# Context and latent keys together in 512-column products, latent values moved to the second phase

## The chip, the cores and the metric

The kernel runs on one core of a Trainium2 chip. The metric is device time in microseconds from start to end of one execution, the median of three runs. Matrix products are done by TensorE (PE, with its weight loads listed apart as PEld). VectorE (DVE) and ScalarE (ACT) split weights and do all elementwise work, GpSimd (POOL) starts some loads and fills borders, SyncE (SP) starts the large loads.

## The reference, cut to what matters

One layer of a hybrid backbone. 256 latent tokens and 256 context tokens, 4096 channels, float32.

```
mod_l = silu(c) @ w_ada + b_ada ;  mod_c = silu(c_ctx) @ w_ada + b_ada     # w_ada: 4096 x 12288
hl = rmsnorm(xl) * (1 + sc_l) + sh_l ;  hc = rmsnorm(xc) * (1 + sc_c) + sh_c
a_val, a_glu, a_gate, r_x, r_gate, q, k, v, c_gate = split(h @ w_in)        # w_in: 4096 x 13312
A: conv module over a_val, a_glu          (latents only)
B: two-way gated recurrence over r_x      (context first, its last state starts the latents)
C: attention of 16 heads, head size 128: q of latents; k, v of latents (windowed) and of context
out = rmsnorm(xl + g_l * (concat(A * silu(a_gate), B * silu(r_gate), C * silu(c_gate)) @ w_out))
```

From the context only r_x (1024 columns), k (2048) and v (2048) are needed; from the latents all nine parts.

## The kernel before, in words

**Products.** A float32 product is made of three passes in float32r. `weights` (L327 to L340) loads up to 4 tiles of 128 contraction rows by 512 output columns (1 MB) through SP's queue into one of 3 buffers `raw`. Then, for two tiles at a time (a pair), ACT copies them into `hi` (L338) and DVE subtracts to `lo` (L339), in 3 buffers each. The activations `h` are kept in two parts likewise. A product adds hi·hi, hi·lo and lo·hi. There are two forms. `gemm_cm` (L342 to L359) is channel-major: the weights are the stationary operand and the 256 tokens of one stream move through, so a matmul has 256 columns; for 512 output columns that is 4 x 3 matmuls of 256 columns for each contraction tile and stream. `gemm_tm` (L361 to L374) is token-major: 128 tokens of `h` are stationary and 512 weight columns move, 3 matmuls of 512 columns for each contraction tile and 128 tokens.

**Phase 1** (L482 to L552) goes over the contraction in blocks of 1, 2, 3, 3, 3, 4, 4, 4, 4, 4 tiles, because the modulation that `h` needs is itself computed during it: units of `w_ada` loads and small products (`ada_units`, L217) are put between the pairs by `background`, at a rate that grows with the weight it is called with. For each block there are ten chunks of 512 columns in the order r0 k0 v0 k1 v1 k2 v2 k3 r1 v3 (in the last block both r first). r is made for both streams by `gemm_cm` (4 PSUM banks), k for the context alone by `gemm_cm` (2 banks), v for both streams by `gemm_tm` (4 banks). `spill` (L499) adds the banks to sums `acc` in SBUF, on DVE. After the ninth chunk of a block, `make_h` (L314 to L324) makes the next block's `h` of both streams, four DVE and two ACT instructions of 256 columns a tile: `CH` for the context, `LH` for the latents.

**Recurrences.** Eight pieces (`recurrence`), one for each head; five are put behind chunks of the last block (`REC1`), three between chunks of the second phase. They share three tiles a direction and two for gate weights.

**Phase 2** (L558 to L742) uses `LH` only, over the whole contraction of 32 tiles: conv inputs (c0, c1), four attention groups of four heads (a0 to a3: k, q, gate, each by `gemm_cm`, then `attention`), gates and pointwise products. In `attention` the scores are two matmuls of 256 keys, context and latents (L593, L594). Phase 3 is the output projection by `gemm_tm`.

**Order and space.** The program orders the instructions of each engine before the run, by priority (`hp` marks what is urgent) and by its own estimate of times; on the chip each engine goes strictly through its list. A tile waits for space until all uses of an earlier tile in its slot are over. SBUF is shared out as 75 pages of 2 KB a partition (X, CH, LH, acc, and nearly every temporary tile) beside the weight buffers. PSUM has 5 banks for the large products and 3 for all else.

Of the kernel before, what the change touches and what calls it, by code (L numbers as in the profile page):

```python
# [10 lines left out]
F32 = mybir.dt.float32  # L11
# [6 lines left out]
P = 128  # L18
D = 4096
KT = D // P  # L20
T = 256
# [4 lines left out]
# blocks of the contraction in the first phase, in tiles of 128  # L26
BLOCKS = [1, 2, 3, 3, 3, 4, 4, 4, 4, 4]
# from this block on, every second one's shift is summed on the vector engine
PAIRED = 8
# pages of 2 KB, buffers of weights as loaded and as split  # L30
NPG, NRAW, NHI = 75, 3, 3
# tiles of the contraction kept for the second half of the last chunk
HELD = 12
# urgency of what the tensor engine waits for
HP = 200000
# rates of the loads that go beside the products, by phase
ADA_A, ADA_B, CAP = 2.15, 1.2, 4.0
G1, G2, G3 = 0.4, 0.3, 0.4
# chunks of the last block that a recurrence follows; order of the second phase
# [5 lines left out]
def tile_hybrid_layer(ctx: ExitStack, tc: tile.TileContext, x, c, cctx_tok, c_ctx, w_ada, b_ada,  # L45
# [13 lines left out]
    def background(weight):  # L59
        """emits queued units of loads between those of the products, at the set rate"""  # L60
        bg["credit"] = min(bg["credit"] + bg["rate"](weight), CAP)
        while bg["q"] and bg["credit"] >= 2.0:
            bg["credit"] -= 2.0
            bg["q"].pop(0)()

    def page(shape, dt=F32, name="pg"):
        uid[0] += 1
        return pg.tile(shape, dt, name=f"{name}_{uid[0]}", tag="pg", bufs=NPG)

# [53 lines left out]
    # silu(c), silu(c_ctx) as channel columns, padded to 32 stationary columns  # L123
# [31 lines left out]
    def accumulate(k, w, n, which):  # L155
        """gacc[b] += silu(vector b)[k] * w on the vector engine"""
# [101 lines left out]
    def rsqrt(y, v, t):  # L258
        """y = v ** -0.5, the table's root refined by a Newton step"""
# [52 lines left out]
    CH, LH = {}, {}  # L312

    def make_h(k):  # L314
        h = page([P, 512], name="h")
        CH[k] = page([P, 2, T], F32R, name="ch")
        LH[k] = page([P, 2, T], F32R, name="lh")
        for s, dst in ((1, CH[k]), (0, LH[k])):
            sl = slice(0, T) if s == 1 else slice(T, 2 * T)
            V.scalar_tensor_tensor(h[:, sl], X[k][:, sl], modG[:, k, s:s + 1], R[:, sl], ALU.mult, ALU.mult)  # L320
            A.activation(dst[:, 0], h[:, sl], AF.Identity, bias=modS[:, k, s:s + 1])
            V.scalar_tensor_tensor(dst[:, 1], h[:, sl], modS[:, k, s:s + 1], dst[:, 0].bitcast(F32),
                                   ALU.add, ALU.subtract)
# [529 lines left out]
```

## Time and profile before

| | us |
|---|---|
| median of 3 runs (2374.56 to 2380.82) | 2377.08 |
| profiled execution, first to last instruction | 2371.5 |
| PE busy | 2315.1 |
| PEld busy | 2034.4 |
| DVE busy | 1580.3 |
| ACT busy | 945.7 |

The profiled execution's time is known as its span, 2371.5 us; the median of the runs is 5.6 us above, which takes in what lies ahead of the first and behind the last instruction. A matmul's row in the trace lasts longer than its distance to the next one, because matmuls are pipelined: what a matmul costs is read from the distance between the starts of successive rows.

### The profile page before, as it was taken

The page shows a single profiled execution, that of the slowest core. Times are in us where ns is not written, and L with a number is a line of the kernel's source. Part 1 is how long each engine was busy: PE and PEld are TensorE (multiplying, and loading weights), DVE is VectorE, ACT ScalarE, POOL GpSimd, SP SyncE. Part 2 cuts the span into 40 slices and gives each one's busy share as a digit, 9 for nine tenths or more (in the row PEclk, how much of TensorE's full clock was granted, in tenths as well). Part 3 has the DMA queues.
Part 4 walks back from the last instruction along what each step waited for, and adds up shares of the span by engine and source line. Part 5 has one row for each costly group of instructions (what it writes and reads, how often), then busy time and mean ns, then how long its engine had stood idle before and what let it go on. Part 6 is the DMA issues. An engine that isn't in the chain of part 4 may idle for free.

```text
span 2371.5 us, 38433 instructions
## 1 busy us (share of the span) xinstructions
PE 2315.1 (98%) x16013; PEld 2034.4 (86%) x16013; DVE 1580.3 (67%) x2289; ACT 945.7 (40%) x1228; POOL 95.8 (4%) x150
## 2 busy tenths in 40 slices
PE   6899999999999999999999999999999999999997
PEld 4667777777788998999999899999999999888886
DVE  4465545445778779987879596955766666665555
ACT  5322212222223246886433343344444434434444
POOL 0000000000000001000000101101001001000000
PEclk9999999999999999999999999999999999999999
DMA  9888788877877544656776767767576678775664
GB/s 312 270 279 272 254 298 298 295 266 252 295 269 258 192 163 174 222 183 213 245 233 203 188 215 202 204 215 188 182 245 171 207 265 301 264 263 187 191 192 173
DMA packets 293461, 551.27 MB, mean 232 GB/s; under 512 B 10959, under 2 KB 52647, under 8 KB 293287
## 3 DMA queue, kind: packets, MB, share of 16 engines
q1 hardware_dynamic: 287856, 536.91, 66.1%
q0 software_dynamic: 4480, 11.54, 4.3%
q8 instruction: 125, 2.05, 0.3%
q10 hardware_dynamic: 951, 0.37, 0.1%
q14 instruction: 49, 0.40, 0.0%
HBM read 544.58 MB, written 4.19 MB: 231 GB/s over the span
## 4 chain that ended last, share of the span: by engine, by line
PE 83%; DMA 8%; DVE 4%; ACT 3%; issue 1%; SPq 0%; DVEq 0%; ACTq 0%
PE gcm L355 48%; PE gtm L371 9%; PE gtm L372 8%; PE gtm L370 8%; PE psa L217 5%; DMA raw<-in_w_ada_dram 4%; DMA raw<-in_w_in_dram 3%; DVE lo L339 2%; PE y L614 1%; ACT hi L338 1%; DMA xp<-in_ctx_dram 1%; DVE gacc L245 1%; PE pt L607 1%; PE sc L593 0%; PE sc L594 0%
## 5 line engine op out<-in xcount | busy, mean ns | idle before, releaser
L339 DVE TENSOR_TENSOR lo<-raw,hi 128x1024 fp32r<-128x1024 f32 (+1 forms) x630 | 747.4, 1189 | 556.8 <-ACT hi L338 552.9
L338 ACT CAST hi<-raw 128x1024 fp32r<-128x1024 f32 (+1 forms) x630 | 640.1, 1022 | 1171.9 <-PE gcm L355 492.8
L355 PE MATMUL gcm<-lh,hi 128*128 128x256 f32 x5632 | 1069.5, 285 | 2.9 <-ACT hi L338 2.8
L355 PEld LDWEIGHTS gcm<-lh,hi 128*128 128x128 f32 x5632 | 896.8, 192 | 18.3 <-issue 13.4
L355 PE MATMUL gcm<-lh,lo 128*128 128x256 f32 x2816 | 796.2, 285 | 4.2 <-DVE lo L339 4.0
L355 PEld LDWEIGHTS gcm<-lh,lo 128*128 128x128 f32 x2816 | 537.8, 192 | 11.6 <-DVE lo L339 5.8
L355 PE MATMUL gcm<-ch,hi 128*128 128x256 f32 x1536 | 326.6, 287 | 3.4 <-ACT hi L338 2.3
L355 PEld LDWEIGHTS gcm<-ch,hi 128*128 128x128 f32 x1536 | 259.0, 191 | 36.3 <-issue 27.8
L245 DVE SCALAR_TENSOR_TENSOR gacc<-raw,scol,gacc 128x512 f32<-128x512 f32 x248 | 185.8, 749 | 49.6 <-DMA raw<-in_w_ada_dram 47.1
L355 PE MATMUL gcm<-ch,lo 128*128 128x256 f32 x768 | 217.6, 286 | 0.0
L371 PE MATMUL gtm<-lo,mix 128*128 128x512 f32 x488 | 192.0, 393 | 0.1
L372 PE MATMUL gtm<-hi,mix 128*128 128x512 f32 x488 | 190.1, 390 | 0.0
L370 PE MATMUL gtm<-hi,mix 128*128 128x512 f32 x488 | 171.1, 390 | 0.0
L355 PEld LDWEIGHTS gcm<-ch,lo 128*128 128x128 f32 x768 | 146.5, 191 | 12.8 <-issue 9.0
L217 PE MATMUL psa<-raw,cpad 128*32 128x512 f32 (+3 forms) x1216 | 132.5, 521 | 7.9 <-DMA raw<-in_w_ada_dram 7.8
L499 DVE TENSOR_TENSOR acc<-acc,gcm 128x512 f32<-128x512 f32 x144 | 96.1, 682 | 37.7 <-PE gcm L355 37.1
L371 PEld LDWEIGHTS gtm<-lo,mix 128*128 128x128 f32 x488 | 91.6, 188 | 20.5 <-DVE lo L339 1.3
L370 PEld LDWEIGHTS gtm<-hi,mix 128*128 128x128 f32 x488 | 91.5, 188 | 19.2
L499 DVE TENSOR_TENSOR acc<-acc,gtm 128x512 f32<-128x512 f32 x144 | 94.3, 680 | 19.9 <-PE gtm L372 19.7
L372 PEld LDWEIGHTS gtm<-hi,mix 128*128 128x128 f32 x488 | 91.7, 188 | 18.4
L673 DVE SCALAR_TENSOR_TENSOR cv<-upad,cols,cv 128x256 f32<-128x256 f32 x240 | 105.6, 483 | 0.0
L371 PE MATMUL gtm<-lo,ch 128*128 128x512 f32 x256 | 102.2, 399 | 0.2 <-DVE lo L339 0.2
(218 smaller groups left out, 2107.9 us busy)
## 6 DMA issues: line engine op xcount, KB each, us to landing
raw<-in_w_in_dram SPq DMA_DIRECT2D x210, 1024.0 KB, 5.2
raw<-in_w_ada_dram SPq DMA_DIRECT2D x156, 1024.0 KB, 5.5
raw<-in_w_out_dram SPq DMA_DIRECT2D x61, 1024.0 KB, 5.5
raw<-in_w_ada_dram SPq DMA_DIRECT2D x48, 768.0 KB, 5.9
raw<-in_w_in_dram SPq DMA_DIRECT2D x30, 768.0 KB, 6.1
raw<-in_w_in_dram SPq DMA_DIRECT2D x10, 512.0 KB, 5.4
xp<-in_ctx_dram SPq DMA_DIRECT2D x16, 256.0 KB, 5.8
xp<-in_x_dram SPq DMA_DIRECT2D x16, 256.0 KB, 5.4
```

What stands on the lines that cost most here:

```text
L217: nc.tensor.matmul(st["ps"][32 * q:32 * q + 32, :W], cpad[k // 16][:, k % 16, :], raw[:, j, :], start=(k < 4), stop=(k >= KT - 4))
L245: V.scalar_tensor_tensor(st["a"], raw[:, j], s, st["a"], ALU.mult, ALU.add)
L338: A.copy(hi[:, :n], raw[:, o:o + n])
L339: V.tensor_sub(lo[:, :n], raw[:, o:o + n], hi[:, :n].bitcast(F32))
L355: nc.tensor.matmul(banks[r // 2][:, (r % 2) * T:(r % 2) * T + T], w[:, j, nt * P:(nt + 1) * P], movs[m][k][:, part], start=first, stop=las ...
L370: nc.tensor.matmul(banks[b], hh, wh[:, j], start=first, stop=False)
L371: nc.tensor.matmul(banks[b], hh, wl[:, j], start=False, stop=False)
L372: nc.tensor.matmul(banks[b], hl, wh[:, j], start=False, stop=last)
L499: V.tensor_add(acc[key, i], acc[key, i], b)
L607: nc.tensor.transpose(ps[:, kt * T + qt * P:kt * T + qt * P + P], Ps[qt][:, (2 * kp + kt) * P:(2 * kp + kt + 1) * P], ident)
L614: nc.tensor.matmul(ps[:, :T], acc[("v", h // 4), kt][:, i * P:(i + 1) * P], Ps[kt // 2][:, (kt % 2) * T:(kt % 2) * T + T], start=(kt == 0) ...
L673: V.scalar_tensor_tensor(o, upad[n][:, tap:tap + T], cw(tap, n), o, ALU.mult, ALU.add)
```

## The change

r and k of phase 1 are made for both streams by one new function, `gemm_both`. The two streams' parts of `h` of one contraction tile now lie side by side in a 4 KB tile `H4` ([part, stream, token]), so that one matmul moves 512 columns. v of phase 1 is made for the context only. In phase 2 each attention group makes the latents' v by `gemm_tm` in the place where it made the latents' k by `gemm_cm`. `keep_h` copies the latents' half of `H4` into a page after the fifth chunk of each block, for phase 2. `make_h` writes its product in place over X. The 4 KB tiles come from six slots of their own (`wide`), which the recurrences' tiles, the padded conv inputs (`upad`) and the attention's probabilities (`pr`) use later; pages go from 75 to 69. The scores become one matmul of 512 keys. The scratch for descriptors of GpSimd's loads is set to 4096.

```diff
-NPG, NRAW, NHI = 75, 3, 3
+NPG, NRAW, NHI, NH4 = 69, 3, 3, 6
...
+    def wide(shape, dt=F32, name="wide"):
+        uid[0] += 1
+        return pg.tile(shape, dt, name=f"{name}_{uid[0]}", tag="wide", bufs=NH4)
...
     def make_h(k):
-        h = page([P, 512], name="h")
-        CH[k] = page([P, 2, T], F32R, name="ch")
+        h = X[k]
+        H4[k] = wide([P, 2, 2, T], F32R, name="h4")
+        CH[k] = H4[k][:, :, 0]
+        for s in (1, 0):
+            sl = slice(0, T) if s == 1 else slice(T, 2 * T)
+            hi, lo = H4[k][:, 0, 1 - s], H4[k][:, 1, 1 - s]
+            V.scalar_tensor_tensor(h[:, sl], h[:, sl], modG[:, k, s:s + 1], R[:, sl], ALU.mult, ALU.mult)
+            A.activation(hi, h[:, sl], AF.Identity, bias=modS[:, k, s:s + 1])
+            V.scalar_tensor_tensor(lo, h[:, sl], modS[:, k, s:s + 1], hi.bitcast(F32), ALU.add, ALU.subtract)
+        del X[k]
+
+    def keep_h(k):
         LH[k] = page([P, 2, T], F32R, name="lh")
+        A.copy(LH[k], H4[k][:, :, 1].bitcast(F32))
...
+    def gemm_both(view, ks, c0):
+        banks = [bank("g", "gcb") for _ in range(4)]
+        for kp, wh, wl in weights(view, ks, c0):
+            for nt in range(4):
+                for j, k in enumerate(kp):
+                    sl = slice(nt * P, (nt + 1) * P)
+                    nc.tensor.matmul(banks[nt], wh[:, j, sl], H4[k][:, 0], start=k == ks[0], stop=False)
+                    nc.tensor.matmul(banks[nt], wh[:, j, sl], H4[k][:, 1], start=False, stop=False)
+                    nc.tensor.matmul(banks[nt], wl[:, j, sl], H4[k][:, 0], start=False, stop=k == ks[-1])
+            background(2)
+        return banks
...
-            rec.extend([page([P, 512], name="rec") for _ in range(3)] for _ in range(2))
-            rec.extend(page([P, 2, 2, P], name="gw") for _ in range(2))
+            t = [wide([P, 2, 512], name="rec") for _ in range(3)]
+            rec.extend([t[d][:, 0], t[d][:, 1], t[2][:, d]] for d in range(2))
+            gws = wide([P, 2, 2, 2, P], name="gw")
+            rec.extend(gws[:, i] for i in range(2))
...
-            if kind == "r":
-                bk = gemm_cm(win, ks, C_RX + 512 * i, [CH, LH])
-            elif kind == "k":
-                bk = gemm_cm(win, ks, C_K + 512 * i, [CH])
+            if kind == "v":
+                bk = gemm_tm(win, ks, C_V + 512 * i, [(CH, 0), (CH, P)])
             else:
-                bk = gemm_tm(win, ks, C_V + 512 * i, [(CH, 0), (CH, P), (LH, 0), (LH, P)])
+                bk = gemm_both(win, ks, (C_RX if kind == "r" else C_K) + 512 * i)
...
+            if ci == 4:
+                for k in ks:
+                    keep_h(k)
...
     def att_group(g):
-        for b in gemm_cm(win, ALLK, C_K + 512 * g, [LH]):
-            t = page([P, 2, T], name="kl")
+        for b in gemm_tm(win, ALLK, C_V + 512 * g, [(LH, 0), (LH, P)]):
+            t = page([P, 512], name="vl")
...
-            nc.tensor.matmul(ps[:, :T], qq, kc, start=True, stop=True)
-            nc.tensor.matmul(ps[:, T:], qq, kl, start=True, stop=True)
+            nc.tensor.matmul(ps, qq, acc[("k", h // 4), i], start=True, stop=True)
...
-                upad[n] = page([P, T + 30], name="upad")
+                if n % 3 == 0:
+                    ups.append(wide([P, 3, T + 30], name="upad"))
+                upad[n] = ups[n // 3][:, n % 3]
...
-    nc = _bacc.Bacc("TRN2", target_bir_lowering=False, num_devices=1)
+    nc = _bacc.Bacc("TRN2", target_bir_lowering=False, num_devices=1, dynamic_dma_scratch_size=4096)
```

## Rows read from the trace of the kernel before

**Rows 1.** The page's first lines: span; busy time, share and count by engine.
```profile
span 2371.5 us, 38433 instructions
PE 2315.1 (98%) x16013; PEld 2034.4 (86%) x16013; DVE 1580.3 (67%) x2289; ACT 945.7 (40%) x1228; POOL 95.8 (4%) x150
```

**Rows 2.** Stretches: length, busy time (count) by engine, granted clock, DMA share, GB/s.
```profile
0.00:80.00 80.00, 54.90 (x510) 42.02 (x510) 34.24 (x79) 44.92 (x106) 3.09 (x13) 0.98 0.94 300
80.00:250.00 170.00, 164.25 (x1112) 118.67 (x1112) 95.18 (x180) 41.45 (x60) 0.00 (x0) 0.98 0.83 272
250.00:550.00 300.00, 299.39 (x1969) 221.93 (x1968) 151.98 (x232) 65.40 (x84) 0.00 (x0) 1.00 0.82 285
550.00:945.00 395.00, 395.00 (x2501) 333.68 (x2500) 300.94 (x432) 128.85 (x155) 10.62 (x20) 1.00 0.65 228
945.00:1320.00 375.00, 371.96 (x2970) 360.52 (x2969) 311.32 (x439) 223.27 (x266) 15.46 (x37) 1.00 0.65 217
1320.00:1380.00 60.00, 55.66 (x412) 53.65 (x411) 41.82 (x69) 25.12 (x38) 10.23 (x12) 0.94 0.67 158
1380.00:1440.00 60.00, 60.00 (x503) 60.00 (x502) 50.90 (x81) 22.14 (x23) 0.00 (x0) 1.00 0.64 224
```

**Rows 3.** Timeline of PE in phase 2: start us, us, instruction; 33 matmuls between these.
```profile
1399.81 0.40 PE L355 MATMUL gcm<-lh,hi 128*128 128x256 f32 x2
...
1403.77 0.40 PE L355 MATMUL gcm<-lh,hi 128*128 128x256 f32 x2
```

**Rows 4.** Timeline of PE in phase 1, a v chunk; 26 matmuls between the last two.
```profile
785.32 0.40 PE L370 MATMUL gtm<-hi,ch 128*128 128x512 f32 x1
...
786.02 0.40 PE L370 MATMUL gtm<-hi,ch 128*128 128x512 f32 x1
...
791.92 0.39 PE L372 MATMUL gtm<-hi,ch 128*128 128x512 f32 x1
```

**Rows 5.** Groups of instructions by form, whole run: count, busy us, mean ns, idle before.
```profile
L355 PE MATMUL gcm<-ch,hi 128*128 128x256 f32 x1536 | 326.6, 287 | 3.4 <-ACT hi L338 2.3 <-ACT ch L321 1.0
L593 PE MATMUL sc<-acc,q 128*128 128x256 f32 x64 | 19.6, 389 | 0.0
L444 PE MATMUL pr<-rec,gw 128*128 128x512 f32 x32 | 16.4, 592 | 0.0
```

**Rows 6.** The same view, DVE and ACT.
```profile
L339 DVE TENSOR_TENSOR lo<-raw,hi 128x1024 fp32r<-128x1024 f32 x590 | 720.7, 1223 | 530.4 <-ACT hi L338 526.6 <-PE pt L607 1.7
L499 DVE TENSOR_TENSOR acc<-acc,gcm 128x512 f32<-128x512 f32 x144 | 96.1, 682 | 37.7 <-PE gcm L355 37.1
L322 DVE SCALAR_TENSOR_TENSOR ch<-h,modS,ch 128x256 fp32r<-128x256 f32 x32 | 15.3, 479 | 3.1 <-ACT ch L321 3.1
L338 ACT CAST hi<-raw 128x1024 fp32r<-128x1024 f32 x590 | 616.5, 1049 | 1135.0 <-PE gcm L355 476.9 <-DMA raw<-in_w_in_dram 332.3 <-PE gtm L372 249.8
L321 ACT ACTIVATE ch<-h,modS 128x256 fp32r<-128x256 f32 x32 | 16.2, 506 | 39.3 <-DVE h L320 25.1 <-DVE modS L183 13.4 <-PE gtm L372 0.8
L497 ACT COPY acc<-gcm 128x512 f32<-128x512 f32 x16 | 8.6, 591 | 3.2 <-PE gcm L355 3.1
L162 DVE SCALAR_TENSOR_TENSOR gacc<-raw,scol,gacc 128x512 f32<-128x512 f32 x62 | 43.1, 744 | 6.7 <-DMA raw<-in_w_ada_dram 6.6
```

**Rows 7.** Single lines: duration ns min/median/max, first and last start us.
```profile
L320 DVE SCALAR_TENSOR_TENSOR h<-xp,modG,R x64: 473/478/486, 46.5 to 754.4; 128x256 f32<-128x256 f32 x64
L432 DVE TENSOR_SCALAR rec<-acc,cols x16: 533/540/547, 850.5 to 1076.5; 128x512 f32<-128x512 f32 x16
L480 DVE TENSOR_TENSOR acc<-rec,rec x8: 411/420/426, 894.1 to 1121.7; 128x256 f32<-128x256 f32 x8
L499 DVE TENSOR_TENSOR acc<-acc,gtm x144: 627/679/690, 105.4 to 941.0; 128x512 f32<-128x512 f32 x144
L663 DVE SCALAR_TENSOR_TENSOR upad<-glu,val x8: 401/418/425, 1048.7 to 1151.9; 128x256 f32<-128x256 f32 x8
```

**Rows 8.** Waits: who waited for whom: us in total, times, longest us.
```profile
POOL B L587 <- DMA B<-in_rpb_dram: 110.7, 15, 9.5
```

More of the change, by code (lines that the diff above doesn't have):

```diff
@@ L310, in tile_hybrid_layer @@
     fin()
-    CH, LH = {}, {}
+    H4, CH, LH = {}, {}, {}
     def make_h(k):
-        h = page([P, 512], name="h")
-        CH[k] = page([P, 2, T], F32R, name="ch")
-        LH[k] = page([P, 2, T], F32R, name="lh")
[L318 to L323, printed above, removed]
-        del X[k]
+        h = X[k]
[9 more added lines that the diff above has]
+    def keep_h(k):
+        LH[k] = page([P, 2, T], F32R, name="lh")
+        A.copy(LH[k], H4[k][:, :, 1].bitcast(F32))
     def weights(view, ks, c0):
@@ L575, in tile_hybrid_layer, with attention @@
     atts = []
-    def attention(h, q, kl, cg):
+    def attention(h, q, vl, cg):
         i = h % 4
-        kc = acc[("k", h // 4), i // 2][:, (i % 2) * T:(i % 2) * T + T]
         if h in (0, 4):
-            atts.append([page([P, 6, 64], name="B"), page([P, 512], name="pr"), page([P, 512], name="pr")])
+            prs = wide([P, 2, 512], name="pr")
+            atts.append([page([P, 6, 64], name="B"), prs[:, 0], prs[:, 1]])
         B3, *Ps = atts[h % len(atts)]
@@ L613, in attention @@
         for kt in range(4):
-            nc.tensor.matmul(ps[:, :T], acc[("v", h // 4), kt][:, i * P:(i + 1) * P],
+            v = acc[("v", h // 4), kt] if kt < 2 else vl[kt - 2]
+            nc.tensor.matmul(ps[:, :T], v[:, i * P:(i + 1) * P],
                              Ps[kt // 2][:, (kt % 2) * T:(kt % 2) * T + T], start=(kt == 0), stop=(kt == 3))
@@ L622, in att_group @@
     def att_group(g):
-        kl, q, cg = [], [], []
-        for b in gemm_cm(win, ALLK, C_K + 512 * g, [LH]):
-            t = page([P, 2, T], name="kl")
+        vl, q, cg = [], [], []
+        for b in gemm_tm(win, ALLK, C_V + 512 * g, [(LH, 0), (LH, P)]):
+            t = page([P, 512], name="vl")
             with hp():
-                A.copy(t.rearrange("p a b -> p (a b)"), b)
-            kl += [t[:, 0], t[:, 1]]
+                A.copy(t, b)
+            vl.append(t)
         aside()
@@ L641, in att_group @@
         for i in range(4):
-            attention(4 * g + i, q[i], kl[i], cg[i])
-    upad, cv = {}, {}
+            attention(4 * g + i, q[i], vl, cg[i])
+    upad, ups, cv = {}, [], {}
     def conv_in(g):
```

## The prediction

> **What bounds the kernel now.** I read the page's first lines, then the stretches, then PE's timeline, then the groups and single lines. TensorE is busy for 2315.1 of 2371.5 us; VectorE for 67% [rows 1]. By stretches PE is idle only at the very start and for short spells: 25 us of the first 80, 6 of the next 170, and from 250 to 945 under 1 us of 695; in phase 2 about 3 of 375 and 4.3 in the stretch from 1320, which also ran at a mean clock of 0.94 [rows 2]. So PE waits for almost nothing, and the time is the sum of the distances between matmul starts. That is where to look, because a busy PE need not be a PE at its peak.
>
> A 256-column matmul costs (1403.77 - 1399.81) / 33 = 0.1200 us [rows 3]; a 512-column one costs (791.92 - 786.02) / 26 = 0.2269 us, in phase 1 itself, with the weights' split and the sums going on beside it [rows 4]. The clock is at its full level, 2.4 GHz, in both stretches (1.00) [rows 2]. Two of 256 therefore cost 0.0131 us more than one of 512: (2 x 0.1200 - 0.2269). Written as a fixed part and a part per column, that is 0.0131 us a matmul and 0.107 us per 256 columns. In the pure 256-column stretch PEld is busy for all 60.00 us; in the phase-1 stretch, which mixes both forms, for 334 of 395 [rows 2].
>
> **The change part by part.**
>
> *Matmul counts.* For a contraction tile of 128: r before is 2 chunks x 4 x 6 = 48 of 256, after 24 of 512. k of the context before is 4 x 4 x 3 = 48 of 256; after, with the latents, 48 of 512. v before is 4 x 4 x 3 = 48 of 512, after 24 of 512. In phase 2 latents' k was 48 of 256 and latents' v is 24 of 512. Columns stay the same; 144 matmuls of 256 become 72 of 512, while v's 48 of 512 are only divided between the phases. Over 32 tiles 4608 matmuls become 2304. The rows agree: 1536 with `hi` are two of three passes of the context's r and k [rows 5], so 2304 in all, and the latents' r and k are as many again.
>
> The gain is 2304 x 0.0131 = 30.2 us: phase 1 goes from 96 x 0.1200 + 48 x 0.2269 = 22.41 to 96 x 0.2269 = 21.78 us a tile, or 20.2 us in all; phase 2 gives 10.0. Bounds for an operation that the trace doesn't have (weights stationary, 512 columns of h moving): the nearest 512-column rows are 0.2269 and, at the head of the same chunk, (786.02 - 785.32) / 3 = 0.2333 [rows 4]. The second would leave 2304 x 0.0067 = 15 us. I take 0.2269, to which the chunk settles within four matmuls.
>
> One page speaks against the gain. The Trainium skill, "TensorE: Matmul & The Clock Gate", section "Back-to-back issue gap", gives an isolated matmul N/2.4 + 2.5 ns; two of 256 against one of 512 would then differ by only 2.5 ns, an estimate from that page of 6 us for all 2304. This trace disagrees: 120.0 and 226.9 ns are 10.8 and 11.1 ns above that formula.
>
> *Loads and their pace.* w_in and w_ada are read as before, chunk for chunk. The weights given to `background` are 2 six times and 1 four times a block before and after; the long and short chunks merely change places. DMA share is 0.82 with 285 GB/s from 250 to 550, against 0.94 and 300 GB/s in the first 80 us [rows 2]: room of about a tenth, while PE asks 3% faster (22.41 / 21.78). In the first 250 us, where PE did wait, I give back half of 6 tiles' gain: 6 x 0.63 / 2 = 2 us. If loads already set the pace up to 550, they would take back more; that is a rival.
>
> *Sums and PSUM.* Banks to be added to `acc`: 8 + 8 + 16 = 32 a block before, 8 + 16 + 8 = 32 after, 0.68 us each on DVE [rows 6]. In the last pair of a four-bank chunk the first bank is done 18 x 0.227 = 4.1 us before the last, so the fifth bank and an early sum keep the next chunk going. Nothing.
>
> *keep_h.* 32 new ACT copies of 512 columns at 0.59 us, by the nearest copy of that size [rows 6]: 19 us on an engine that is busy for 129 of 395 us there [rows 2]. Hidden; if one stood right ahead of a late `hi` it would cost 0.6 us. Writing h over X costs nothing: the same instructions.
>
> *Six wide slots.* This is a new wait. A block of 4 tiles holds 4 slots, so `make_h` can prepare two tiles of the next block early; the other two must wait until the last chunk (v3) is through with its first pair. Before, `h` was made long ahead: the last L320 began at 754.4 [rows 7]. From that release PE has v3's second pair, 12 x 0.227 = 2.7 us, and the next chunk's first pair, 24 x 0.227 = 5.4 us: 8.1 us. Needed in it on ACT: four `hi` parts of 0.51 and the next pair's `hi`, 1.05: 3.1 us. On DVE: the instruction just running (1.2), four `lo` parts of 0.48, two sums of 0.68 and the next `lo`, 1.22: 5.7 us [rows 6]. It fits with 2.4 us to spare. Queued behind the waiting instructions on ACT and DVE are those splits, and PE waits for them. Where a batch of vector-summed modulation lies ahead (8 x 0.744 = 6.0 us for a load [rows 6]), it would overrun by 3.6 us. There are five such boundaries (the one from 3 to 4 tiles waits for a single tile): 0 to 18 us; I take 0.5 each, 2.5 us, because the program can order around a wait that it foresees.
>
> *Recurrences.* They need four wide slots; in the last block only two are free, so the first can't finish before phase 1's end, 941.0 [rows 7] less 20 = 921. Before, the first ended at 894.1 and the eighth at 1121.7, one every 32.5 us [rows 7]. After: 921 + 8 x 32.5 = 1181. The last two padded conv inputs need a slot of theirs, so they come at 1181 instead of 1152 [rows 7]. PE doesn't wait for them: conv results are used after the third attention group, hundreds of us on, and DVE is free for 64 of 375 us there [rows 2]. The price is pages held meanwhile, a rival below. Bounds from -5 (the DVE-heavy end of phase 1 eased) to +60; I take 0.
>
> *Phase 2 otherwise.* Two score matmuls of 256 become one of 512. The 256-column score row lasts 389 ns and the 512-column row of the gate products 592 [rows 5], each listed twice for a matmul; 32 of them, within 5 us either way; 0. The gate and recurrence tiles, upad and pr leave the pages (8 + 8 + 4 tiles) for the wide slots, against 6 pages taken away, which may ease the 4.3 us stall and the 3.6 us of lost clock from 1320 [rows 2]. Not counted. GpSimd's smaller scratch touches loads such as the bias rows, which POOL awaited for 7.4 us each (110.7 / 15) [rows 8]; doubled they are still POOL's, idle for 96% [rows 1]. Nothing.
>
> Sum against the profiled span: 2371.5 - 30.2 + 2 + 2.5 = 2345.8. With the 5.6 us between span and median, 2351.
>
> **Rivals.**
>
> *Early loads set the pace.* DVE's sums of v run from 105.4 to 941.0 [rows 7], for some 30 tiles, 28 us each; so 470 / 28 = 17 tiles go through from 80 to 550, and their 17 x 0.63 = 10.7 us would be lost, 9 more than counted: 2360. For it: DMA share 0.82 to 0.83 there. Against it: PE idle of 0.6 us from 250 to 550 [rows 2].
>
> *The new form costs more than the old one.* At 0.2333 a matmul the gain is 15 us: 2366; dearer still, as if only 2.5 ns a pair were left, 6 us: 2375 with my 4.5 us of losses. For it: the head of the chunk [rows 4]. Against it: 26 matmuls behind it. The page's formula named above would end there too.
>
> *Phase 2 gains from looser pages.* Stall and clock loss from 1320 go, with a like amount at the later attention groups: 12 us more, 2339. For it: pages are what B, pr and upad wait for in the code. Against it: an attention start needs four fp32 steps in a row anyway.
>
> *Slower: late recurrences hold the pages.* At the start of phase 2, 64 of 69 pages are LH and acc. Until the last recurrence is over, vals, glu, cv, the latents' v and then q need about 9, with 5 free and 3 given back by finished recurrences. q comes at 921 + 4 x 46 + 44 + 46 = 1195, just behind 1181. If each recurrence takes 43 us, as the first did (850.5 to 894.1 [rows 7]), the eighth ends at 1265: PE stands for up to 70 us, 2415. Even at 36.5 us (1213) it costs 18 us. It decides from about 38 us each (1225, 30 us), where the gain is gone. Against it: recurrences have precedence over the convs in the order, and DVE is freer once the sums end.
>
> **How the numbers follow.** Forecast 0.55 (2345 to 2359). Early loads 0.13; dearer form 0.09, of which 0.04 within no change; looser pages 0.13; late recurrences 0.10, of which 0.07 slower and 0.03 no change. What a measurement can tell from no change is 0.3%, 7 us: faster is under 2370, slower over 2384. Faster 0.55 + 0.13 + 0.05 + 0.13 = 0.86; for boundaries that go wrong together (18 us, and more in the worst order) I move 0.03 of it to no change and 0.01 to slower: 0.82, 0.10, 0.08. The range 2337 to 2371 takes in looser pages and the dearer form, and leaves out the stalled cases.
>
> **What would show it.** Right: matmuls of gcb 0.227 us apart, about 2304 fewer rows of PE, phase 1's last sum near 921, PE busy for all but a few us of each block boundary. Wrong: gaps of PE behind the last v chunk of a block, waits of L499's successors or of `hi` for `make_h`; PE idle at the first attention group with recurrences still running past 1195; or gcb matmuls 0.233 us and more apart.

## The result, and the profile after

The changed kernel takes 2395.57 us (2392.03 to 2397.49), the kernel before 2376.40 (2374.56 to 2380.82), four runs each on one chip: ratio 1.0074 [1.0058, 1.0089], 19.2 us slower. The forecast was 2351, 25 us faster, with a range of 2337 to 2371: the result lies outside the range and on the other side of the kernel before, a case that the prediction had given a chance of 0.08.

The page's first lines after, and its shares of the chain that ended last, the work followed back from the last instruction (they answer to [rows 1]):

```profile
span 2393.5 us, 33658 instructions
...
PE 2307.5 (96%) x13645; PEld 1902.5 (79%) x13645; DVE 1579.0 (66%) x2289; ACT 958.7 (40%) x1260; POOL 91.4 (4%) x150
...
PE 77%; DMA 12%; DVE 7%; ACT 3%; issue 1%; POOL 0%; SPq 0%; ACTq 0%; DVEq 0%; POOLq 0%
```

The same chain line of the kernel before:

```profile
PE 83%; DMA 8%; DVE 4%; ACT 3%; issue 1%; SPq 0%; DVEq 0%; ACTq 0%
```

PE lost 2368 rows, as many as the merge should take away (2304, and 64 of the scores, which are listed twice), but only 7.6 us of busy time, and the span is 22 us longer: PE now waits. In that chain PE's share falls by 6 points, while DMA's rises by 4 and VectorE's by 3.

The stretches after (columns as in [rows 2]) show where. The last four are short stretches around the attention groups:

```profile
80.00:250.00 170.00, 159.67 (x842) 102.49 (x842) 93.33 (x178) 47.65 (x72) 0.00 (x0) 0.98 0.80 260
250.00:550.00 300.00, 294.10 (x1455) 188.71 (x1453) 149.99 (x235) 67.81 (x93) 0.00 (x0) 1.00 0.83 280
550.00:945.00 395.00, 390.91 (x1818) 297.05 (x1815) 279.15 (x391) 104.98 (x125) 6.11 (x22) 1.00 0.70 239
1140.00:1200.00 60.00, 55.24 (x297) 47.55 (x296) 50.80 (x79) 31.80 (x36) 3.55 (x8) 0.94 0.70 212
1320.00:1380.00 60.00, 54.53 (x277) 44.65 (x276) 35.92 (x55) 23.27 (x37) 9.61 (x11) 0.97 0.78 217
1500.00:1560.00 60.00, 56.37 (x347) 51.14 (x346) 46.07 (x82) 22.70 (x31) 10.12 (x12) 0.94 0.80 203
1740.00:1800.00 60.00, 55.74 (x437) 54.58 (x436) 41.80 (x62) 28.20 (x41) 4.21 (x4) 0.94 0.64 198
```

From 80 to 945 PE is idle for 20.3 us, against 6.4 before [rows 2]; in each of the four short stretches it stands for 3.6 to 5.5 us and then runs for a while at a lower clock. The matmuls themselves are as forecast. PE's timeline in an r or k chunk of phase 1 (the new operation; ten matmuls between the two starts):

```profile
799.74 0.39 PE L379 MATMUL gcb<-h,hi 128*128 128x512 f32 x1
...
802.01 0.39 PE L380 MATMUL gcb<-h,lo 128*128 128x512 f32 x1
```

(802.01 - 799.74) / 10 = 0.227 us, the spacing of [rows 4].

To place the loss, the ends of the stages (us) are read from PE's timeline of each kernel, by counting the columns of the large products. Two experiments from below stand beside them: `e16_before_late` is the kernel before with a lighter load of the bias rows and with recurrences as late as after; `e8_even_bias` is the changed kernel with that load and with a fixed rate of `w_ada` units.

| end of | before | after | e16 | e8 | e8 - e16 |
|---|---|---|---|---|---|
| block 0 | 86.0 | 92.0 | 87.2 | 84.7 | -2.5 |
| block 2 | 244.0 | 248.8 | 245.0 | 246.6 | +1.6 |
| phase 1 | 940.4 | 940.0 | 932.1 | 923.9 | -8.2 |
| conv inputs | 1147.7 | 1158.9 | 1152.3 | 1139.4 | -12.9 |
| group a0 | 1286.8 | 1303.0 | 1293.4 | 1277.4 | -16.0 |
| group a1 | 1451.8 | 1464.7 | 1449.7 | 1431.5 | -18.2 |
| group a2 | 1613.8 | 1628.3 | 1605.2 | 1584.6 | -20.6 |
| group a3 | 1777.0 | 1800.2 | 1768.4 | 1753.5 | -14.9 |
| last output chunk | 2358.8 | 2380.8 | 2348.6 | 2336.2 | -12.4 |

The last row is of one profiled execution each: there `e8` is 12.4 us ahead of `e16`, by the medians 16.7.

Before against after: phase 1, where 20 us were to be gained, ends at the same time, although the last block's recurrences have left it. The conv inputs then lose 11.6, and the four groups another 12.0.

### The profile page after: what moved, and what is told of

Same layout as the page of the kernel before. It is cut to its first block, busy times and chain, and to the rows that moved or that the text cites. A ratio compares the mean times of both kernels' runs of the same rounds, so it can differ in the third digit from the quotient of the medians.

```text
span 2393.5 us, 33658 instructions
## 1 busy us (share of the span) xinstructions
PE 2307.5 (96%) x13645; PEld 1902.5 (79%) x13645; DVE 1579.0 (66%) x2289; ACT 958.7 (40%) x1260; POOL 91.4 (4%) x150
## 3 DMA queue, kind: packets, MB, share of 16 engines
q0 software_dynamic: 4480, 11.54, 4.3%
## 4 chain that ended last, share of the span: by engine, by line
PE 77%; DMA 12%; DVE 7%; ACT 3%; issue 1%; POOL 0%; SPq 0%; ACTq 0%; DVEq 0%; POOLq 0%
PE gcm L365 26%; PE gtm L394 8%; PE gtm L395 8%; PE gtm L393 7%; PE gcb L378 6%; PE gcb L380 6%; PE gcb L379 6%; DMA raw<-in_w_ada_dram 6%; DMA raw<-in_w_in_dram 5%; PE psa L222 4%; DVE lo L349 3%; ACT hi L348 2%; PE y L640 1%; PE sc L619 1%; DVE gacc L250 1%
## 5 line engine op out<-in xcount | busy, mean ns | idle before, releaser
L349 DVE TENSOR_TENSOR lo<-raw,hi 128x1024 fp32r<-128x1024 f32 (+1 forms) x630 | 750.8, 1195 | 507.6 <-ACT hi L348 505.5
L365 PE MATMUL gcm<-lh,hi 128*128 128x256 f32 x4096 | 754.7, 287 | 9.1 <-ACT hi L348 4.8
L365 PEld LDWEIGHTS gcm<-lh,hi 128*128 128x128 f32 x4096 | 643.0, 193 | 17.8 <-issue 7.2
L365 PE MATMUL gcm<-lh,lo 128*128 128x256 f32 x2048 | 582.0, 287 | 5.7 <-DVE lo L349 5.7
L365 PEld LDWEIGHTS gcm<-lh,lo 128*128 128x128 f32 x2048 | 393.1, 193 | 11.4 <-DVE lo L349 7.3
L378 PE MATMUL gcb<-h,hi 128*128 128x512 f32 x768 | 306.1, 401 | 2.4 <-ACT hi L348 1.3
L379 PE MATMUL gcb<-h,hi 128*128 128x512 f32 x768 | 303.5, 395 | 0.0
L380 PE MATMUL gcb<-h,lo 128*128 128x512 f32 x768 | 287.8, 397 | 0.0
L524 DVE TENSOR_TENSOR acc<-acc,gcb 128x512 f32<-128x512 f32 x216 | 144.1, 682 | 114.1 <-PE gcb L380 113.8
L378 PEld LDWEIGHTS gcb<-h,hi 128*128 128x128 f32 x768 | 145.3, 189 | 62.3 <-issue 23.0
L380 PEld LDWEIGHTS gcb<-h,lo 128*128 128x128 f32 x768 | 144.4, 188 | 57.2 <-issue 22.6
L379 PEld LDWEIGHTS gcb<-h,hi 128*128 128x128 f32 x768 | 145.1, 189 | 43.9 <-issue 15.3
L394 PE MATMUL gtm<-lo,lh 128*128 128x512 f32 x256 | 103.2, 403 | 5.3 <-DVE lo L349 5.3
L393 PEld LDWEIGHTS gtm<-hi,mix 128*128 128x128 f32 x488 | 91.6, 188 | 19.2
```

Of the source, the lines that this page charges most:

```text
L349: V.tensor_sub(lo[:, :n], raw[:, o:o + n], hi[:, :n].bitcast(F32))
L365: nc.tensor.matmul(banks[r // 2][:, (r % 2) * T:(r % 2) * T + T], w[:, j, nt * P:(nt + 1) * P], movs[m][k][:, part], start=first, stop=las ...
L378: nc.tensor.matmul(banks[nt], wh[:, j, sl], H4[k][:, 0], start=k == ks[0], stop=False)
L379: nc.tensor.matmul(banks[nt], wh[:, j, sl], H4[k][:, 1], start=False, stop=False)
L380: nc.tensor.matmul(banks[nt], wl[:, j, sl], H4[k][:, 0], start=False, stop=k == ks[-1])
L393: nc.tensor.matmul(banks[b], hh, wh[:, j], start=first, stop=False)
```

## The experiments

The edits are shown shortened. Ratios are to the kernel before on the same chip, with 95% intervals; it took 2373.9 to 2374.5 there. The changed kernel was timed on the first chip only, so differences to it are of medians from two chips; by the ratios they come out 2 to 5 us otherwise (`e1` 10.5, `e2` 29.7, `e4` 25.9).

**First four: which part is it?** Theories: loads set the pace of phase 1 since the chunks changed places; or the merge itself isn't worth what it should be; or the exchange of k and v does the harm; or GpSimd's bias rows in phase 2.

`e1_split`: the changed kernel with each matmul of `gemm_both` made as two of 256 columns again, all else kept.

```diff
-  matmul(banks[nt], w, H4[k][:, part])
+  for m in range(2): matmul(banks[nt][:, m*T:m*T+T], w, H4[k][:, part, m])
```

> The changed kernel (2395.6 us) with each 512-column matmul of gemm_both issued as two of 256, all else alike. If the wider matmul is worth 0.0131 us a pair wherever it stands and PE sets the pace: 2304 x 0.0131 = 30 us slower, 2426. If loads set the pace in blocks 0 to 7 (24 of 32 tiles), the 24 x 0.94 = 23 us there are hidden and some 8 us remain: 2404. If the wide form brings nothing at all: 2396.

Measured 2403.38, ratio 1.0118 [1.0094, 1.0143]. So in the changed kernel the merge is worth 7.8 us and not 30: most of what it saves is waited away elsewhere.

`e2_even`: the changed kernel with a fixed credit per pair of tiles. A unit of `w_ada` costs 2 credits and at most 4 are kept. With 3.1 for a long chunk (r, k) and 0.95 for a short one, the old order gave one unit after each pair at the start of phase 1; the new order puts long chunks side by side and soon gives two, none, two, none.

```diff
-  lambda w: ADA_A * w - ADA_B if len(done) + 1 < len(BLOCKS) else G1 * w
+  lambda w: 2.025 if len(done) + 1 < len(BLOCKS) else G1 * w
```

> The changed kernel with a fixed 2.025 credits a pair for the modulation's loads, in place of 3.1 for long and 0.95 for short chunks; the sum over a long and a short chunk is the same. If the lumps in the order of loads (two of w_ada, then two of w_in) cause the lost time of blocks 0 to 7: 10 to 17 us back, 2380. If the short v pairs (2.7 us) as such, or the six wide slots, cost it: 2392 to 2398.

Measured 2364.15, 0.9949 [0.9932, 0.9965]: 31 us below the changed kernel, more than either expectation had, though no matmul is different. Phase 1 ends at 923.9. The stretches of `e2_even`, with idle time of 0.3 and 1.4 us where the changed kernel has 5.9 and 4.1:

```profile
250.00:550.00 300.00, 299.66 (x1489) 199.00 (x1485) 156.44 (x240) 73.50 (x97) 0.00 (x0) 1.00 0.80 276
550.00:945.00 395.00, 393.60 (x1892) 299.77 (x1891) 277.23 (x386) 117.08 (x141) 7.18 (x24) 1.00 0.68 238
```

SP's queue shows the lumps. Its timeline in the changed kernel, in the first block (start, us, the load that SP issues, how many):

```profile
65.53 1.00 SPq L217 DMA_DIRECT2D raw<-in_w_ada_dram  x2
66.63 5.76 SPq L342 DMA_DIRECT2D raw<-in_w_in_dram  x2
75.83 1.00 SPq L217 DMA_DIRECT2D raw<-in_w_ada_dram  x2
```

and the same place in the kernel before, where they come one by one:

```profile
62.06 0.38 SPq L212 DMA_DIRECT2D raw<-in_w_ada_dram  x1
63.07 0.33 SPq L332 DMA_DIRECT2D raw<-in_w_in_dram  x1
63.49 0.39 SPq L212 DMA_DIRECT2D raw<-in_w_ada_dram  x1
68.45 0.33 SPq L332 DMA_DIRECT2D raw<-in_w_in_dram  x1
```

That difference lasts for the first blocks only. Further on both kernels have runs of three, first the kernel before, then the changed one:

```profile
300.19 7.45 SPq L212 DMA_DIRECT2D raw<-in_w_ada_dram  x3
...
408.23 6.44 SPq L217 DMA_DIRECT2D raw<-in_w_ada_dram  x3
```

Counted in SP's timeline from 250 to 550, both issue 57 `w_ada` loads in 29 runs, 11 of three before and 12 after. `e2_even` issues 54, and only one run of three.

What such a run does to PE in the changed kernel is seen in its chain, behind the second of these lines (start, us, what):

```profile
416.88 1.04 PE psa L222 x8
...
417.93 6.63 DMA raw<-in_w_in_dram
...
424.66 1.05 ACT hi L348
...
425.73 1.24 DVE lo L349
...
427.01 0.50 PE gtm L394
```

A `w_in` load could only be issued when the `w_ada` products had given a buffer back; it took 6.6 us, then come `hi` and `lo`, and PE meanwhile ran out of work (it is idle for 1.4 us between 424 and 427). The kernel before has such runs too and is idle for only 0.6 us in these 300.

`e3_noswap`: only r is merged; k of the context and v of both streams stay in phase 1 and k of the latents in phase 2, all in their old forms; the wide slots are kept.

```diff
-  bk = gemm_both(...)                                   # k
+  bk = gemm_cm(win, ks, C_K + 512 * i, [CH])
-  bk = gemm_tm(..., [(CH, 0), (CH, P)])                 # v
+  bk = gemm_tm(..., [(CH, 0), (CH, P), (L4, 0), (L4, P)])
```

> The changed kernel with k and v left where they were (k of the context by 256 columns, v of both streams in phase 1, k of the latents in phase 2); only r is merged, and the wide slots, 69 pages and the later recurrences stay. If the swap (its load order and its short v chunks) costs the time: faster than before by r's 768 x 0.0131 = 10 us, 2366 to 2370. If slots, pages and recurrences cost it: 2385 to 2400.

Measured 2384.61, 1.0040 [1.0025, 1.0055]: 11 us better than the whole change, and still slower than before. The exchange is a part, not the whole.

`e4_bias`: the changed kernel with the bias rows of a head loaded as one run of 219 numbers for each of 64 partitions, instead of six overlapping runs of 64, and spread out by the mask product on GpSimd, in six instructions instead of one.

```diff
-  G.dma_start(B3[64*rl:64*rl+64], AP(..., ap=[[1, 64], [31, 6], [1, 64]]))
-  G.tensor_mul(B3, B3, mask[:, 0:1]...)
+  G.dma_start(Bt[64*rl:64*rl+64, 0:219], AP(..., ap=[[1, 64], [1, 219]]))
+  for r in range(5, -1, -1): G.tensor_mul(B3[:, r], Bt[:, 31*r:31*r+64], mask[:, 0])
```

> The changed kernel with the bias rows loaded as one run of 219 numbers a partition and spread by GpSimd (128 descriptors a head in place of 768). If the bias loads clog the DMA engines and starve PE in phase 2: the stalls of 5.2, 4.1, 3.9 and 4.5 us and half of their 20 us at half clock, up to 25 us: 2370 to 2380. If the stalls there come from pages or from VectorE's order: 2390 to 2398.

Measured 2366.52, 0.9965 [0.9952, 0.9978]: 29.1 us below the changed kernel, all of it in phase 2. The first three of the four stretches have no idle time and the full clock in `e4_bias`:

```profile
1140.00:1200.00 60.00, 60.00 (x331) 51.85 (x330) 56.43 (x87) 33.46 (x38) 8.15 (x13) 1.00 0.67 229
1320.00:1380.00 60.00, 60.00 (x362) 52.22 (x361) 43.62 (x69) 27.54 (x42) 16.66 (x27) 1.00 0.60 202
1500.00:1560.00 60.00, 60.00 (x463) 57.38 (x462) 45.70 (x72) 28.06 (x40) 17.14 (x23) 1.00 0.64 215
```

The fourth stall is another matter. In the changed kernel PE's wait there ends with ACT's copy `vl`:

```profile
1754.48 0.80 PE L365 MATMUL gcm<-lh,hi 128*128 128x256 f32 x2 [4.26 <-ACT vl L653]
```

GpSimd issues no bias load from 1715 to 1760, and `e4_bias` has the same wait, 27 us earlier, in group a3:

```profile
1727.20 0.79 PE L365 MATMUL gcm<-lh,hi 128*128 128x256 f32 x2 [4.24 <-ACT vl L655]
```

`e14_norm_last` below shows where it comes from.

POOL's wait for the load in the changed kernel (it answers to [rows 8]; us in total, times, longest):

```profile
POOL B L613 <- DMA B<-in_rpb_dram: 113.5, 15, 9.4
```

and in `e4_bias`:

```profile
POOL B L615 <- DMA B<-in_rpb_dram: 44.5, 15, 5.3
```

How the old load stops PE can be followed at 1165 in the changed kernel. First five-microsecond stretches (columns as above): from 1165 on the DMA engines are busy for 0.91 of the time and move 32 GB/s; from 1175 PE stands, and then it runs at 0.50 of the clock, the 1.2 GHz level.

```profile
1160.00:1165.00 5.00, 5.00 (x23) 4.13 (x23) 4.50 (x12) 3.35 (x5) 0.00 (x0) 1.00 0.86 296
1165.00:1170.00 5.00, 5.00 (x23) 4.14 (x23) 5.00 (x10) 1.69 (x2) 1.32 (x2) 1.00 0.91 32
...
1175.00:1180.00 5.00, 0.88 (x4) 0.38 (x2) 2.09 (x4) 0.00 (x0) 1.99 (x2) 0.91 0.72 273
1180.00:1185.00 5.00, 4.36 (x10) 3.47 (x11) 5.00 (x9) 1.05 (x1) 0.00 (x0) 0.50 0.14 17
```

POOL's timeline there (both halves of a bias tile, issued from 1165.57):

```profile
1165.57 1.32 POOL L610 DMA_DIRECT2D B<-in_rpb_dram  x2 [23.80 <-DVE cv L701]
```

The chain behind it (start, us, what):

```profile
1166.95 10.93 DMA raw<-in_w_ada_dram
1177.88 0.02 issue
1177.91 0.04 DVE gacc L250
1177.94 0.63 issue
1178.57 0.87 DVE cv L701 x2
1179.45 1.15 DVE lo L349
1180.59 0.04 issue
1180.64 0.80 PE gtm L394
```

The `w_ada` load beside the bias rows takes 10.9 us. An instruction of VectorE (`gacc`) waits for it; the `lo` that PE needs stands behind it in VectorE's list. At the stalls behind 1369 and 1524 the late load is `w_in` itself, of 9.5 and 11.6 us, and PE waits for it by way of ACT.

**Second four: does the same hold before the change, and how much is the loads?**

`e5_before_bias`: the kernel before with the bias rows as in `e4_bias`.

> The kernel before with the bias rows loaded as one run of 219 numbers a partition. If bias loads starve PE there too: its two stalls of 4.6 and 3.1 us and half of 10 us at half clock, up to 13 us: 2363 to 2370. If they don't: 2376.

Measured 2360.42, 0.9942 [0.9927, 0.9957]: 13.5 us. The kernel before had the fault too, at two places: the stall from 1320 in [rows 2] and a second one, here in the kernel before:

```profile
1500.00:1560.00 60.00, 57.00 (x432) 55.51 (x431) 48.30 (x77) 26.90 (x37) 11.03 (x10) 0.97 0.72 209
```

Both are gone in `e5_before_bias`; its stretch from 1320:

```profile
1320.00:1380.00 60.00, 60.00 (x473) 58.95 (x473) 44.71 (x74) 27.18 (x40) 16.16 (x27) 1.00 0.61 197
```

The old bias rows cost 13.5 us before and 29.1 after the change (13.8 and 25.9 by the ratios).

`e6_half` and `e7_before_half`: half of each `w_ada` unit in the first two thirds is loaded and each half is used twice, in the changed kernel and in the one before. These kernels leave out half of those weights, so their sums are not the reference's; the matmuls are as many.

```diff
-  S.dma_start(raw, wada[:, kg:kg + kk, ...])
+  S.dma_start(raw[:, :kk//2], wada[:, kg:kg + kk//2, ...])
   ... matmul reads raw[:, j % (kk//2), :]
```

> The changed kernel with half of the first two thirds of w_ada loaded (each loaded half is used twice, so the modulation's sums are not the reference's); matmul counts as before. Read against the kernel before with the same cut. If loads set the pace of blocks 0 to 7, phase 1 now shows the full gain of the wide matmuls: about 18 us less than the kernel before with the same cut. If slots, make_h or the short v chunks cost the time, the changed kernel stays level with it or behind it in phase 1.

> The kernel before with half of the first two thirds of w_ada loaded, each loaded half used twice. If loads cost it little (PE idle under 10 us from 80 to 945): 2355 to 2370. It is the yardstick for the changed kernel with the same cut.

Measured 2355.63 (0.9925 [0.991, 0.9939]) and 2350.74 (0.9907 [0.9891, 0.9924]): 40 us less for the changed kernel, 23 for the one before. So both wait for loads, the changed one for more: the time from the end of block 2 to the end of phase 1 falls from 696.4 to 694.7 us before and from 691.2 to 675.6 after. With half the bytes phase 1 ends at 900.0 in the changed kernel and at 918.4 in the old one: 18.4 apart, where with all the bytes there was no difference. The stretch from 250 to 550 of `e6_half` has no idle time:

```profile
250.00:550.00 300.00, 300.00 (x1483) 194.29 (x1483) 153.36 (x232) 73.62 (x99) 0.00 (x0) 1.00 0.58 191
```

`e8_even_bias`: the changed kernel with both edits, fixed rate and light bias rows.

> The changed kernel with both the fixed rate for the modulation's loads and the bias rows in runs of 219. If each loss is its own and both theories hold: 15 + 15 us back, 2355 to 2370. If only one holds: 2375 to 2385.

Measured 2348.28, 0.9893 [0.9879, 0.9908]: the forecast's figure, reached only with two edits that the change doesn't have.

**Third four: is it the rate, its evenness, or the order?**

`e9_scaled`: the changed kernel, its uneven rate times 0.904, so that the mean of the credits given per pair is the 2.025 of `e2_even`. The cap of 4 takes some of them away again: from 250 to 550 it issues 51 `w_ada` loads against 54 of `e2_even` and 57 of the changed kernel, and 12 runs of three.

```diff
-  ADA_A * w - ADA_B if ...
+  0.904 * (ADA_A * w - ADA_B) if ...
```

> The changed kernel with the modulation's rates scaled by 0.904 (2.80 credits for a long pair, 0.86 for a short one): the same sum over ten chunks as the fixed 2.025 that brought it to 2364, but as uneven as before. If a lower pace of loads is what helped: 2362 to 2368. If the even spacing is what helped: 2385 to 2396.

Measured 2379.81, 1.0026 [1.0016, 1.0036], between the two expectations: roughly half of the 31.4 us is the lower rate (15.8; 11.4 by the ratios) and the rest the evenness. Since the scaled rate is the lower of the two, the split is not exact.

`e10_before_even` and `e11_before_even_bias`: the kernel before with the fixed rate, without and with light bias rows.

> The kernel before with the fixed 2.025 credits a pair. If the rates suited its order of chunks and the change spoilt them: 2372 to 2378, no gain. If the rates were too high or uneven for it as well: 2358 to 2366, and the changed kernel's 2364 is no gain of the change.

> The kernel before with the fixed rate and the bias rows in runs of 219: the yardstick for the changed kernel with both (2348). If the change is worth its matmul spacing less what phase 2 still loses: 2358 to 2366. If the fixed rate also helps the kernel before: 2345 to 2352.

Measured 2395.94 (1.0094 [1.0076, 1.0112]) and 2363.39 (0.9957 [0.9943, 0.9971]). Before the change the fixed rate is no gain: 22 us worse, which neither expectation had, or level with `e5_before_bias` once the bias rows are light (3 worse, within the noise); its phase 1 ends at 944.1 and 941.5 instead of 940.4 and 939.9. So the uneven rate suited the old kernel and doesn't suit the new one. The pairs of runs that differ by the bias rows alone give their price: 13.5 and 32.6 us in the kernel before with its own and with the fixed rate (`e10`, `e11`), 29.1, 23.0 and 15.9 in the changed one with its own, the scaled (`e15` below) and the fixed rate (`e2`, `e8`). So how hard the bias rows hit hangs on the rate in phase 1, and with it on where the other loads lie around them.

`e12_split_even_bias`: `e8_even_bias` with each merged matmul as two of 256 again.

> The changed kernel with the fixed rate and the bias runs (2348), and each 512-column matmul of gemm_both issued as two of 256. With loads out of the way PE should set the pace of phase 1: 2304 x 0.0131 = 30 us slower, 2374 to 2380. If phase 1 is still set by loads: 2350 to 2362.

Measured 2373.83, 0.9998 [0.9988, 1.0008]: where loads don't hold PE, the merge is worth 25.5 us by the medians (20.3 by the profiled spans; 19.2 in phase 1, 943.1 to 923.9). Beside `e1` it also shows what the new order of chunks does alone: with matmuls of 256 columns phase 1 ends at 945.0 with the uneven rate (`e1`) and at 943.1 with the fixed one, 2 us apart; with merged matmuls at 940.2 and 923.9 (`e4`, `e8`), 16 apart. (Single profiles with the same phase 1 end it within 4 us of each other: 923.2 to 923.9 in `e2`, `e8` and `e14`, 933.7 and 937.5 in `e3` and `e13`.) The uneven loads hold back a faster PE, and hardly one of the old speed.

**Last four: what is left between before and after?** With light bias rows in both, the kernels still differ by 6 us the wrong way. Candidates: the exchange of k and v, the rate, the recurrences that come later, and the conv layer norm beside group a3.

`e13_noswap_bias`: `e3_noswap` with light bias rows.

> k and v left where they were, r alone merged, wide slots kept, and the bias rows in runs of 219; the yardstick is the kernel before with the same bias loads (2360). If slots, pages and late recurrences cost nothing: 768 x 0.0131 = 10 us less, 2350. If they cost what the changed kernel lacks (18 us): 2366 to 2370.

Measured 2367.27, 0.9968 [0.9958, 0.9979]: the upper of the two expectations. Phase 1 ends at 937.5 (at 933.7 in the profile of `e3`, whose phase 1 is the same), later than in `e16` (932.1), though r's 768 matmuls fewer should give 768 x 0.0131 = 10 us. Up to 932 its PE is idle for 38.2 us, against 29.4 in `e16` (sums over the stretches), 34.8 of it in the first 250. At the start its loads come one by one as in the kernel before, so the twos aren't the reason here. From 80 to 250 none of PE's waits ends with a part of `h` from `make_h`, the longest in sum (3.6 us) ends with `w_ada` loads. That a faster PE comes sooner to where it waits for loads fits this, but slots, pages and recurrences are changed in this kernel too and were not tried one by one.

`e14_norm_last`: `e8_even_bias` with the conv layer norm after group a3 instead of before it.

```diff
-ORDER = "c0 c1 a0 a1 a2 n a3".split()
+ORDER = "c0 c1 a0 a1 a2 a3 n".split()
```

> The changed kernel with the fixed rate and the bias runs (2348), with the conv branch's layer norm behind the last attention group in place of ahead of it. If its burst on VectorE and ScalarE costs the 9 us of stalls in that group's chunks: 2340. If it stalls the gate chunks behind just as much: 2346 to 2352.

Measured 2342.33 (2341.27 to 2343.82), 0.9867 [0.9845, 0.9888]: 6.0 us better than `e8_even_bias` (the intervals just overlap, the single times don't), and the fastest version of all, 1.3% under the kernel before. The stretch of a3 in `e8_even_bias`, with 3.4 us of idle time:

```profile
1585.00:1755.00 170.00, 166.63 (x1097) 152.19 (x1096) 114.02 (x167) 80.07 (x116) 27.78 (x46) 0.98 0.57 191
```

and `e14_norm_last`, without idle time:

```profile
1585.00:1755.00 170.00, 170.00 (x1172) 156.69 (x1171) 105.49 (x133) 72.26 (x94) 26.91 (x45) 1.00 0.64 212
```

The kernel before has its norm in the same place and no idle time:

```profile
1585.00:1755.00 170.00, 170.00 (x1347) 167.47 (x1346) 113.05 (x161) 80.07 (x113) 15.33 (x17) 1.00 0.67 198
```

This is the fourth stall from above: 4.26 us in the changed kernel, 4.24 in `e4`, 3.4 in `e8`, each ending with the copy `vl`. With matmuls of 256 columns it stays (4.25 in `e1`, 3.36 in `e12`); without the exchange of k and v (`e3`, `e13`) it is gone. So the exchange brings it, not the merge.

`e15_scaled_bias`: the changed kernel with the rates times 0.904 and light bias rows.

> The changed kernel with the scaled uneven rate and the bias runs; against 2348 with the fixed rate and 2367 with the rates as changed. If the pace alone matters, with the bias loads out of the way: 2346 to 2352. If evenness matters by itself: 2356 to 2364.

Measured 2356.82, 0.9929 [0.991, 0.9948]: with the bias rows out of the way the lower rate gives 9.7 us and evenness another 8.5, 18.2 together, split as roughly as in `e9`.

`e16_before_late`: `e5_before_bias` with the five recurrences of the last block put behind phase 1, as late as the changed kernel has them.

```diff
-REC1 = (1, 2, 4, 6, 8)
+REC1 = ()             # and aside(5) behind the block loop
```

> The kernel before with the bias runs (2360), with its first five recurrences put behind phase 1 in place of inside its last block. If late recurrences are what the changed kernel lacks: 8 to 12 us slower, 2369 to 2372. If VectorE has room for them in phase 2: 2358 to 2363.

Measured 2364.95, 0.9962 [0.9947, 0.9977]: late recurrences cost 4.5 us, hardly clear of the noise (the intervals overlap). Phase 1 ends 7.8 earlier than in `e5` (932.1 against 939.9) and the conv inputs 5.0 later (1152.3 against 1147.3).

## Why the prediction was wrong, step by step

The way from before to after in steps between two kernels, by medians:

| step | from, to | forecast | measured |
|---|---|---|---|
| bias rows made light | before, e5 | | -13.5 |
| recurrences as late as after | e5, e16 | 0 | +4.5 |
| merge and exchange, `w_ada` at a fixed rate | e16, e8 | -25.7 | -16.7 |
| `w_ada` rate as in the change | e8, e4 | 0 | +18.2 |
| bias rows as in the change | e4, after | | +29.1 |

The two steps of the bias rows belong together: 29.1 - 13.5 = 15.6 us (12.1 by the ratios), forecast 0. The sum is 21.6: the measured 19.2 and 2.5 between the kernel before on two chips. It closes by construction; what the runs show is the size of each step.

**Matmul spacing: right, and not wholly received.** Forecast 0.2269 a matmul; measured 0.227. The 30.2 us came to 25.5 (`e12` to `e8`) where the fixed rate feeds PE, and to 7.8 (`e1`) in the changed kernel as it is. Phase 2's share came: groups a0 to a2 gain 3.1, 2.2 and 2.4 us in the table's last column, against 2.5 forecast for each. The rival of a dearer form is out. By its formula for isolated matmuls the Trainium skill's page "TensorE: Matmul & The Clock Gate" (section "Back-to-back issue gap") would have two of 256 columns cost 2.5 ns more than one of 512, an estimate from it of 6 us for 2304; `e12` shows 25.5, so the trace and the run disagree with it.

**"In the first 250 us ... I give back": mis-sized.** 2 us were given back. `e8` is idle there for 37.0 us (24.9 of the first 80 and 12.1 of the next 170), `e16` for 29.2: 7.8 more. From 80 to 250 the waits that end with a `w_ada` load are 8.6 us in `e8` and 1.4 in `e16`. Block 2 ends 1.6 later in `e8` than in `e16`, where six tiles should have gained 3.8: 5.4 us, nearly half of the 12.0 by which phase 1 falls short of 20.2 (8.2 in the table). The size is uncertain: single profiles of kernels with the same phase 1 as `e8` are idle for 34.8 (`e2`) and 33.1 us (`e14`), the kernel before for 30.9.

**"Loads and their pace": this step failed, 18 us.** It said that loads come "chunk for chunk" as before and that "the long and short chunks merely change places", with room of about a tenth for a PE that asks 3% faster. The bytes are the same, but at the pace that was set for the old kernel the loads can't follow the faster PE. Shown by `e4` to `e8`: 2366.52 - 2348.28 = 18.2 us with no matmul changed, 16.3 of it in phase 1 (940.2 to 923.9), while the same fixed rate gains nothing in the kernel before (`e5` to `e11`). The new order of chunks alone is not the reason: with matmuls of 256 columns the rate is worth 2 us in phase 1 (`e1`, `e12`), with merged ones 16. Roughly half is the lower rate (`e15`), the rest evenness. Both kernels issue runs of three `w_ada` loads ahead of a `w_in` load, as many as there are `raw` buffers; the fixed rate has almost none. Which of these runs stops PE, and why only at the new speed, was followed at one place (416 to 427) and is otherwise argued. The rival "early loads set the pace" had the mechanism, but priced it at 9 us and only up to 550; after has 4.1 us of idle time behind 550 too, against none before. A mean DMA share of 0.82 [rows 2] was read as room, and it says nothing on when a load lands that waits in SP's list for a buffer.

**GpSimd's loads, "Nothing": this step failed, 15.6 us.** They were costed by the engine that issues them, idle for 96%. The price falls on the other loads, and PE pays it by way of VectorE or ACT. It stood in the rows: the stall from 1320 [rows 2] was put down to pages, and it is gone in `e5`, which frees no page. The rows add up to the price: before, the stretches from 1320 and 1500 have 4.3 + 3.0 us of idle time and lose 60 x (0.06 + 0.03) = 5.4 us of clock, 12.7 of the 13.5; after, the three from 1140, 1320 and 1500 have 13.9 and 9.0, 22.9 of the 29.1 (25.9 by the ratios). Why it hits harder after the change can only be argued: the loads around it lie elsewhere. The price varies with the rate alone from 13.5 to 32.6 us in the kernel before and from 15.9 to 29.1 in the changed one, so neither the merge nor the smaller scratch is needed to explain it. The smaller scratch was not tried by itself; POOL's wait is 113.5 / 15 = 7.6 us each after, 7.4 before.

**Recurrences "taken at 0": 4.5 us**, within the bounds and hardly clear of the noise. The last came at 1157.1, ahead of the 1181 forecast (duration ns, first and last start):

```profile
L505 DVE TENSOR_TENSOR acc<-rec,rec x8: 417/424/426, 965.1 to 1157.1; 128x256 f32<-128x256 f32 x8
```

The slower rival, late recurrences that hold the pages, did not come true: (1157.1 - 965.1) / 7 = 27.4 us each, below the 34 at which it would begin to cost ((1195 - 921) / 8). (The rival's 2415 adds its 70 us to the forecast span; by the median it would be 2421.) What slowed the kernel was in none of the rivals on that side.

**Phase 1's end.** Forecast 921 for the last sum; it began at 942.9. In `e8` the products end at 923.9.

**Wide slots and looser pages.** 2.5 us were charged for the slots; from 80 on no wait of PE in the changed kernel ends with a part of `h`, the wait that was feared; `e12` has one of 2.7 us. Pages gave nothing that shows: with light bias rows PE has no wait over 1 us at the starts of the groups.

**Not thought of: the conv layer norm.** Beside a3, where 2.5 us were to be gained, `e8` gives back 5.7 (20.6 to 14.9). PE's wait there ends with ACT's copy of the latents' v out of PSUM, which stands behind the norm's pieces on ACT and VectorE; the norm after a3 takes the stall away and gains 6.0 (`e14`). The kernels without the exchange of k and v have the norm in the same place and no such stall, so the change brought it. Whether a later norm would also gain something in the kernel before was not tried.

**Still open.** Some 7 of the 12.0 us missing in phase 1 of `e8` (5.4 are lost by the end of block 2): behind 250 its PE has only 1.4 us of idle time up to 945. Also why the waits in the first 250 us grow by more than a faster PE gains there, in `e13` too; how much slots and pages have to do with that; and whether merged matmuls in the old order of chunks would fare better.

## What to carry to other kernels

When an engine is busy for 98% and a change shortens its work, ask whether the loads that feed it, at the pace and in the sequence in which they are issued, can follow the faster engine, and not only how many bytes they are. A pace that was set for the slower engine has to be set again (here 18 to 31 us, as much as the merge itself was worth). Cost a load by what it does to the others on the DMA engines, not by the idle engine that issues it. And a short stall in the profile of before is worth an experiment of its own ahead of a forecast: it may be the place that the change makes worse.

## What the hardware showed unexpectedly

- A load of bias rows in short runs keeps the DMA engines busy for 0.91 of a stretch and moves 32 GB/s (1165 to 1170); a `w_ada` load beside it takes 10.9 us. As longer runs, POOL's wait for the load falls from 7.6 to 3.0 us each (113.5 / 15, 44.5 / 15), and the DMA queue's share of the engines from 4.3% to 1.6%, with 1.35 MB less in it (11.54 and 10.19 MB). The queue's row of after (packets, MB, share of 16 engines):

```profile
q0 software_dynamic: 4480, 11.54, 4.3%
```

and of `e4_bias`:

```profile
q0 software_dynamic: 3968, 10.19, 1.6%
```

- Behind pauses of PE of 3.6 to 4.8 us in phase 2 came a spell at 1.2 GHz (clock 0.50 from 1180 to 1185, after a pause that began at 1175.9), so that a pause costs more than its length: the three stretches of after that the bias rows hit have 13.9 us of idle time together, and 60 x (0.06 + 0.03 + 0.06) = 9.0 us of clock are lost in them. `e4_bias` has neither there.
- The rate at which loads are put between the products moves the kernel by 1% to either side, with the same bytes and the same matmuls: the same fixed rate makes the changed kernel 31 us faster and the old one 22 slower.
